# Twelve block products of a feed-forward layer ahead of its activation sums, with the memory pools around them laid out anew

## The chip, the cores and the metric

The kernel runs on one core of a Trainium2 chip. The metric is the device time of one execution in microseconds (us); the time before is the median of three runs. Engines are named as in the profile: PE is TensorE's matmul (PEld its weight load), DVE is VectorE, ACT is ScalarE, POOL is GpSimd, SP is SyncE, which here only issues transfers. L1197 is line 1197 of the kernel before.

## What is computed

One decoder layer over 1024 tokens of width 1024, all in float32. A token mixer (two groups of attention heads) ends in an output projection; its result is normalised, scaled and added to the input. A SwiGLU feed-forward with 2816 hidden features follows. Of the reference, the part that matters here:

```
y = concat(o_a, o_b) @ w_out
x = x + ga_m * rms_norm(y) * g_post_mix
h = rms_norm(x) * g_pre_ffn * (1 + sc_f) + sh_f
gate, up = split(h @ w_gate_up)
x = x + ga_f * rms_norm((silu(gate) * up) @ w_down) * g_post_ffn
```

## The kernel before

**Float32 as pairs.** Every matrix operand is split into a high part (a cast, L118 on ACT or L120 on DVE/POOL) and a low part (the difference, L121, on DVE or POOL). A product of two such operands takes three matmuls (hi·hi, hi·lo, lo·hi), each 128x128 weights on 512 columns.

**The planner.** The program is written as a sequence of tile operations. A planner with a cost model puts them into one fixed order per engine: among the operations that it takes to be ready, the one written first goes first. Each engine's queue then runs in that order, and the transfers that an engine issues stand in its queue too (SP most loads, ACT the `yd` loads and the stores). A tile waits until the earlier holders of its buffer, or of the same addresses, are done.

**Memory.** Pools lie on two stacks, `L` from the left and `R` from the right. During the last attention part (its `dsa_` pools fill most of `R`) the left stack already holds `fraw` (7 raw weight tiles), `fsum` (4 weight sums) and `fab0` (4 split weight blocks), then `outp`. `h2` (5 spaces of 16 KB per partition) lies on `R`, over the addresses of the attention's `dsa_hi`, which is used to the end of attention.

**The front stage** (L1069 to L1153) runs from the end of attention to the feed-forward:
- `WO`: the second half of w_out, 8 loads of 256 KB (L1092), split into the spaces `s1`, `s2` of `h2`.
- Eight token tiles (loop at L1103). For each: load the other half's result `yd` and `x`; split the attention output (`ohl`, into space `s4`); 24 matmuls into one bank of `ps_S` and one of `ps_O` (2 and 3 banks); two adds (L1120), two squares on ACT (L1121), small statistics and a power on POOL, multiplication with the gate `G_m` (L1125, mostly POOL), the update (L1129) and its store to `x2d`, a third square (L1131), and the scaling by 1/rms (L1133, DVE). `yt` has two buffers (space `s3`), `xt` five.
- After tile 3, eight transposed and modulated rows (`mod`, L1101, ACT) give the float32 copy `HB` and the split blocks `B11`, `B21` of the first 512 tokens.
- After tile 7, four steps k (L1142 to L1152) make the sums of a Strassen-Winograd scheme from both token halves: per step two `mod`, three sums on DVE, one on POOL, and five splits into `T1` to `T4` and `B22`.

**The feed-forward's first part** (L1156 to L1248, here called the main loop). For each of 22 feature tiles f, seven block products named "1" to "7" replace eight, each 12 matmuls (L1197). Their weights are two raw halves of gate, two of up, and four sums of them made on POOL (L1175 to L1178, `sources`); `prepare` splits a block 8 products ahead (ACT, DVE) into `fab0` (4 buffers) or `fab1` (6). Products "1" and "2" are gate times `B11` and `B21`: they need no sum, neither of weights nor of activations. "1" leaves a partial result `p1`, "2" completes it and gives silu of the first token half. The other five take `T2`, `T3`, `T1`, `T4`, `B22`. In `order` the "1" and "2" of f = 0 and 1 stand first. Each f stores 512 KB of `actd`.

**The second part** (the down projection, L1256 on) loads w_down (`wdr`, L1268) and `actd` (`adr`), splits them into `wd` and `ac`, and multiplies. Its pools `dw`, `da`, `dr`, `df` go on the left stack after `fraw` to `fca` are gone, `dr` over the lower end of `h2`, where `T3`/`T4` lie.

Of the kernel before, what the change touches and what calls it, by code (L numbers as in the profile page):

```python
# [13 lines left out]
P = 128  # L14
# [33 lines left out]
def hybrid_layer(ctx, tc, x, c, w_ada, b_ada, g_pre_mix, g_post_mix, g_pre_ffn, g_post_ffn, w_in,  # L48
# [1023 lines left out]
    fab = [L.push("fab0"), None]  # L1072
    op_ = L.push("outp")
# [5 lines left out]
    def space(tag):  # L1079

        return h2p.tile([P, 4096], F32, name="sp" + tag, tag=tag)

    WO = [space("s1").bitcast(F32R), space("s2").bitcast(F32R)]
    WO = [w.rearrange("p (k j d) -> p k j d", k=2, j=2) for w in WO]
    sp3, sp4 = space("s3"), space("s4")
    rawo = sp3[:, 0:2048].rearrange("p (b d) -> p b d", b=4)
# [8 lines left out]
    x2s = []  # L1095
    HB = op_.tile([P, KT, 512], F32, name="HB")
# [6 lines left out]
    for t in range(NT):  # L1103
# [3 lines left out]
        xt = op_.tile([P, D], F32, name="xt2", bufs=5)  # L1107
# [27 lines left out]
        if t == 3:  # L1135
            for k in range(KT):
                mod(HB[:, k, :], k, tr_k(x2s, k))
                b = (B11, B21)[k // KH_]
                split(b[:, k % KH_, 0, :], b[:, k % KH_, 1, :], HB[:, k, :], V, V if k % 2 else G)
    B22 = block(otp[1], "o")  # L1140
    T1, T2, T3, T4 = (block(h2p, "s%d" % j) for j in (1, 2, 3, 4))
    for k in range(KH_):  # L1142
        tm = [op_.tile([P, 512], F32, name=f"tm{j}") for j in range(6)]
        b12, b22, t1, t2_, t3, t4 = tm
        mod(b12, k, tr_k(x2s[4:], k))
        mod(b22, k + KH_, tr_k(x2s[4:], k + KH_))
        V.tensor_tensor(t1, b12, HB[:, k, :], op=OP.subtract)
        V.tensor_tensor(t2_, b22, t1, op=OP.subtract)
        G.tensor_tensor(t3, b22, b12, op=OP.subtract)
        V.tensor_tensor(t4, HB[:, k + KH_, :], t2_, op=OP.subtract)  # L1150
        for b, src, e in ((T2, t2_, V), (T3, t3, G), (T1, t1, V), (T4, t4, V), (B22, b22, G)):
            split(b[:, k, 0, :], b[:, k, 1, :], src, S, e)  # L1152
# [7 lines left out]
    FAB = (4, 6)  # L1160
# [3 lines left out]
    srcs, blks = {}, {}  # L1164

    def sources(f):

        r = {}
        for u in range(2):
            for h in range(2):  # L1170
                r[u, h] = fraw.tile([P, KH_, P], F32, name="rawg", bufs=7)
                nc.sync.dma_start(r[u, h], w_gate_up[0, h * 512:(h + 1) * 512, u * DFF + f * P:u * DFF + (f + 1) * P]
                                  .rearrange("(a p) n -> p a n", a=KH_))
        s1, s2, s3, s4 = (fsum.tile([P, KH_, P], F32, name=f"sw{j}") for j in range(4))
# [6 lines left out]
    def prepare(n):  # L1181
# [5 lines left out]
        b = int(n % sum(FAB) >= FAB[0])  # L1187
        blk = fab[b].tile([P, 2, KH_, P], F32R, name="wgu", bufs=FAB[b])
# [3 lines left out]
    def product(bank, n, w):  # L1192

        blk, hb = blks.pop(n), HBK[w]
        for k in range(KH_):
            for a, b in ((0, 0), (0, 1), (1, 0)):
                PE.matmul(bank, blk[:, a, k, :], hb[:, k, b, :], start=w in "165" and k + a + b == 0,  # L1197
                          stop=k == KH_ - 1 and a == 1, skip_group_check=True)

    def half_t(name, nb):  # L1200
        return fca.tile([P, 512], F32, name=name, bufs=nb)

    st_ = {}
# [3 lines left out]
    for n, (f, w) in enumerate(order):  # L1207
        prepare(n + LOOK)
        q = st_.setdefault(f, {})
        if w == "1":  # L1210
            q["X"] = ps_S()
            product(q["X"], n, w)
            q["p1"] = half_t("p1", 3)
            S.copy(q["p1"], q["X"])
        elif w == "2":
            product(q["X"], n, w)
            q["act"] = fca.tile([P, SEQ], F32, name="act", bufs=3)
            S.activation(q["act"][:, 0:512], q["X"], AF.Silu)
        elif w == "6":
            q["Z"] = ps_T()  # L1220
            product(q["Z"], n, w)
            q["u2"] = half_t("u2", 2)
            V.tensor_tensor(q["u2"], q["Z"], q["p1"], op=OP.add)
        elif w == "7":
            product(q["Z"], n, w)
            q["u3"] = half_t("u3", 2)
            V.tensor_tensor(q["u3"], q["Z"], q["p1"], op=OP.add)
        elif w == "5":
            q["W"] = ps_O()
            product(q["W"], n, w)  # L1230
# [12 lines left out]
        if w == "3" and f == 3:  # L1243
            acc5 = fca.tile([P, D], F32, name="act", bufs=3)
            with low(ADALOW):
                ada_acc(5, acc5, fraw, "rawg", 512, 7, nc.sync)
        if w == "3" and f == 6:
            ada_sum(5, acc5)  # L1248
    for name in ("fca", "fab1", "fab0", "fsum", "fraw"):
        L.pop(name)  # L1250
# [112 lines left out]
```

## Time and profile before

| | us |
|---|---|
| median of 3 runs (lowest, highest) | 1627.02 (1625.99, 1630.45) |
| profiled execution, its own time | 1627.21 |
| its span, first to last instruction | 1625.3 |
| PE busy | 1480.6 (91% of the span) |
| DVE, ACT, POOL busy | 1105.2, 847.9, 791.0 |

The profiled execution's time is 1.9 us more than its span, and 0.2 us from the median. Matmuls are pipelined: one that shows 389 ns starts 0.227 us after the one before it, so starts, not durations, tell the pace.

### The profile page before, as it was taken

How to read it: one execution, taken by the hardware profiler on the slowest of the kernel's cores; microseconds unless marked ns; L12 is line 12 of the kernel's file. 1: busy time of each engine (PE TensorE's matmuls, PEld its weight loads, DVE VectorE, ACT ScalarE, POOL GpSimd, SP SyncE). 2: the span in 40 equal slices, each digit the busy share in tenths (PEclk: the TensorE clock that was granted, in tenths of full speed). 3: DMA queues.
4: the chain of work that ended last, by engine and by line, in shares of the span. 5: the costliest groups of instructions: out<-in, count | busy, mean ns of one | idle time of the engine just before them, and what ended most of it. 6: DMA issues, size and time to landing. Idle time of an engine off the chain costs nothing. (4 is left out here: it accounts for less than half of the span.)

```text
span 1625.3 us, 23560 instructions
## 1 busy us (share of the span) xinstructions
PE 1480.6 (91%) x7973; PEld 1254.0 (77%) x7973; DVE 1105.2 (68%) x2476; ACT 847.9 (52%) x1802; POOL 791.0 (49%) x1046
## 2 busy tenths in 40 slices
PE   3899999987899998999978469999999998999998
PEld 3788999986677877788867358788888886888886
DVE  6888898989989997788746685845445453424422
ACT  3547588857778777778644443223323322432421
POOL 2584344548776655465536665544444442422320
PEclk9999999998999999999989679999999999999999
DMA  9461341200000002101253212622222214744721
GB/s 305 146 213 27 86 124 56 64 7 7 10 8 1 12 1 87 39 33 53 79 188 129 91 52 91 192 79 80 85 78 85 78 52 162 259 143 151 245 78 65
DMA packets 119913, 151.88 MB, mean 93 GB/s; under 512 B 15648, under 2 KB 83584, under 8 KB 119664
## 3 DMA queue, kind: packets, MB, share of 16 engines
q1 hardware_dynamic: 105856, 118.94, 23.6%
q10 hardware_dynamic: 13296, 29.30, 5.0%
q0 software_dynamic: 640, 2.13, 0.4%
q8 instruction: 63, 1.03, 0.3%
q14 instruction: 58, 0.48, 0.1%
HBM read 122.25 MB, written 28.09 MB: 93 GB/s over the span
## 5 line engine op out<-in xcount | busy, mean ns | idle before, releaser
L1197 PE MATMUL pT<-hbs,wgu 128*128 128x512 f32 x792 | 192.5, 393 | 16.9 <-ACT wgu L118 14.1
L1197 PEld LDWEIGHTS pT<-hbs,wgu 128*128 128x128 f32 x792 | 149.8, 190 | 49.8 <-ACT wgu L118 14.5
L742 DVE TENSOR_TENSOR ptl<-pT,ptl 128x512 fp32r<-128x512 f32 x228 | 139.5, 626 | 29.3 <-ACT ptl L741 28.1
L121 DVE TENSOR_TENSOR wd<-wdr,wd 128x512 fp32r<-128x512 f32 x88 | 68.3, 822 | 105.9 <-ACT wd L118 105.4
L741 ACT CAST ptl<-pT 128x512 fp32r<-128x512 f32 x228 | 117.5, 540 | 38.8 <-PE pO L842 17.6
L118 ACT CAST wgu<-sw 128x512 fp32r<-128x512 f32 x88 | 53.9, 621 | 145.8 <-PE pT L1197 81.6
L272 PE MATMUL pO<-wsp,hT 128*128 128x256 f32 (+1 forms) x416 | 121.2, 293 | 7.6 <-DVE hT L120 2.6
L273 PE MATMUL pO<-wsp,hT 128*128 128x256 f32 (+1 forms) x416 | 120.6, 291 | 5.1 <-DVE wsp L121 5.1
L274 PE MATMUL pO<-wsp,hT 128*128 128x256 f32 (+1 forms) x416 | 120.0, 289 | 0.0
L825 POOL TENSOR_SCALAR p<-p,stat,gates 128x640 f32<-128x640 f32 (+7 forms) x128 | 106.2, 843 | 23.2 <-DVE stat L737 17.7
L121 POOL TENSOR_TENSOR ac<-adr,ac 128x512 fp32r<-128x512 f32 x44 | 61.5, 1399 | 112.8 <-ACT ac L118 110.4
L732 ACT ACTIVATE p<-p,stat 128x640 f32<-128x640 f32 (+7 forms) x128 | 93.9, 736 | 26.7 <-DVE stat L731 17.2
L118 ACT CAST wd<-wdr 128x512 fp32r<-128x512 f32 x88 | 50.2, 619 | 102.6 <-PE pO L274 78.6
L121 DVE TENSOR_TENSOR wgu<-sw,wgu 128x512 fp32r<-128x512 f32 x88 | 78.7, 903 | 33.0 <-ACT wgu L118 27.2
L1235 POOL TENSOR_TENSOR act<-act,p 128x512 f32<-128x512 f32 x22 | 36.8, 1673 | 128.7 <-DVE p L1234 112.4
L538 ACT ACTIVATE tk_j<-scores,tk_s 128x384 bf16<-128x384 f32 (+2 forms) x93 | 87.1, 936 | 11.0 <-DVE tk_s L480 3.5
L272 PEld LDWEIGHTS pO<-wsp,hT 128*128 128x128 f32 x416 | 81.9, 198 | 9.3 <-ACT wsp L118 2.7
L273 PEld LDWEIGHTS pO<-wsp,hT 128*128 128x128 f32 x416 | 82.0, 198 | 6.7 <-DVE wsp L121 5.8
L121 DVE TENSOR_TENSOR wgu<-rawg,wgu 128x512 fp32r<-128x512 f32 x66 | 61.1, 929 | 36.9 <-ACT wgu L118 36.8
L470 DVE TENSOR_SCALAR_CACHE_REDUCE tk_j<-scores,tk_v 128x512 bf16<-128x512 f32 (+2 forms) x96 | 83.9, 874 | 1.1 <-DMA mkd<-tk_j 0.5
L721 PE MATMUL pS<-KK,qst 128*128 128x512 f32 (+3 forms) x192 | 76.1, 402 | 8.3 <-DVE stat L729 7.9
L837 PE MATMUL pT<-ident,p 128*128 128x128 f32 x528 | 81.7, 277 | 1.7 <-DVE ptl L742 1.2
(465 smaller groups left out, 4661.3 us busy)
## 6 DMA issues: line engine op xcount, KB each, us to landing
rawg<-in_w_gate_up_dram SPq DMA_DIRECT2D x88, 256.0 KB, 3.0
wdr<-in_w_down_dram SPq DMA_DIRECT2D x44, 512.0 KB, 5.1
actd<-act ACTq DMA_DIRECT2D x22, 512.0 KB, 2.6
adr<-actd SPq DMA_DIRECT2D x44, 256.0 KB, 3.6
raw<-in_w_in_dram SPq DMA_DIRECT2D x36, 256.0 KB, 2.9
xt<-in_x_dram SPq DMA_DIRECT2D x16, 512.0 KB, 5.7
wt<-in_w_ada_dram SPq DMA_DIRECT2D x32, 256.0 KB, 4.5
wt<-in_w_ada_dram SPq DMA_DIRECT2D x16, 512.0 KB, 5.0
```

The lines of the kernel that those rows point to most:

```text
L118: S.copy(hi, src)
L121: elo.tensor_tensor(lo, src, hi.bitcast(F32), op=OP.subtract)
L272: PE.matmul(o, lh, rh, start=first, stop=False)
L273: PE.matmul(o, lh, rl, start=False, stop=False)
L274: PE.matmul(o, ll, rh, start=False, stop=last)
L470: V.tensor_scalar(tkj[0][:, :w], score(i0 + j), thr(j), 0.0, op0=op, op1=OP.add, accum_out=cnt[:, j:j + 1])
L538: S.activation(tkj[1][:, :(i0 + j + 1) * P], score(i0 + j), AF.Sign, bias=ff[:, j:j + 1], accum_out=sg[:, j:j + 1])
L732: S.activation(p_, p_, AF.Exp, bias=stat[:, 0, r:r + 1], scale=-1.0, accum_out=stat[:, 1, r:r + 1])
L741: S.copy(hl[:n_rows, 0, :width], src[:n_rows, :width])
L742: V.tensor_tensor(hl[:n_rows, 1, :width], src[:n_rows, :width], hl[:n_rows, 0, :width].bitcast(F32), op=OP.subtract)
L825: G.tensor_scalar(self.p4[:, r, :n], self.p4[:, r, :n], stat[:, 2, r:r + 1], gates[:, i, c0 + r:c0 + r + 1], op0=OP.mult, op1=OP.mult)
L1197: PE.matmul(bank, blk[:, a, k, :], hb[:, k, b, :], start=w in "165" and k + a + b == 0, stop=k == KH_ - 1 and a == 1, skip_group_check=True)
```

## The change

- `early(f)`, for f = 0 to 5: products "1" and "2" of six feature tiles are written into the front stage, three among token tiles 5 to 7, three among the steps k = 0 to 2. Both results (`pr`, a tile of 512 KB) are stored to `early_d` in DRAM and loaded back as `p1` and `act` when the main loop comes to f. `order` is then five products for f < 6 and seven for the others: 142 in place of 154.
- `WO`, and after it `T1` and `B22`, get a pool of their own, `sl`, on the left stack under `outp`; `ohl` uses `fab0`'s buffers, which the early weights share; w_out's raw tiles use `fraw`; `yt` (and the sums' temporaries) three buffers `tm` in `outp`.
- The gate multiplication is one DVE operation per tile, the 1/rms scaling goes from DVE to ACT, `HB`'s splits go to ACT and DVE, the sums are written in place and all on DVE, and every split there is ACT and DVE; `WO`'s low parts are all on POOL.
- In the second part `dw` goes on the right stack, `dr` lowest on the left, then `da` and `df`.
- The ada columns (16 loads, DVE work) move from f = 3 and 6 to f = 8 and 11.

```diff
+    sl = L.push("sl")
     op_ = L.push("outp")
...
+    def wblock(b=0):
+        return fab[b].tile([P, 2, KH_, P], F32R, name="wgu", bufs=FAB[b])
+    def raw_w():
+        return fraw.tile([P, KH_, P], F32, name="rawg", bufs=7)
+    def pair():
+        return fsum.tile([P, 2, 512], F32, name="pair", bufs=2)
+    FAB = (4, 6)
+    EARLY = 6
+    early_d = dram.tile([EARLY, P, 2, 512], F32, name="earlyd")
-    WO = [space("s1").bitcast(F32R), space("s2").bitcast(F32R)]
+    WO = [sl.tile([P, 2, 2, D], F32R, name="WO" + tag, tag=tag) for tag in ("s1", "s2")]
...
-            raw = rawo[:, (2 * k + j) % 4, :]
+            raw = raw_w().rearrange("p a b -> p (a b)")
-            split(WO[k // 2][:, k % 2, 0, d], WO[k // 2][:, k % 2, 1, d], raw, S, V if k % 2 else G)
+            split(WO[k // 2][:, k % 2, 0, d], WO[k // 2][:, k % 2, 1, d], raw, S, G)
...
-        yt = sp3[:, 2048 + 1024 * (t % 2):3072 + 1024 * (t % 2)]
+        yt = op_.tile([P, D], F32, name="tm", bufs=3)
-        ohl = sp4[:, 1024 * (t % 2):1024 * (t % 2) + 1024].bitcast(F32R).rearrange("p (j k q) -> p j k q", j=2, k=4)
+        ohl = wblock()
-            e = V if j and t % 2 == 0 else G
-            e.tensor_tensor(yt[:, d], yt[:, d], G_m[:, d], op=OP.mult)
+        V.tensor_tensor(yt, yt, G_m, op=OP.mult)
-        V.tensor_scalar(xt, xt, r2, None, op0=OP.mult)
+        S.activation(xt, xt, AF.Copy, scale=r2)
...
+    def weights(n):
+        f, h = n // 2, n % 2
+        raw = raw_w()
+        nc.sync.dma_start(raw, w_gate_up[0, h * 512:(h + 1) * 512, f * P:(f + 1) * P]
+                          .rearrange("(a p) n -> p a n", a=KH_))
+        blk = wblock()
+        split(blk[:, 0], blk[:, 1], raw, S, V)
+        return blk
+    def early(f):
+        ws = [weights(2 * f + h) for h in range(2)]
+        bank = ps_O() if f % 2 else ps_S()
+        pr = pair()
+        product(bank, ws[0], B11, True, False)
+        S.copy(pr[:, 0], bank)
+        product(bank, ws[1], B21, False, True)
+        S.activation(pr[:, 1], bank, AF.Silu)
+        nc.scalar.dma_start(early_d[f], pr)
+    for t in range(4):
+        out_tile(t)
+    for k in range(KT):
+        mod(HB[:, k, :], k, tr_k(x2s, k))
+        b = (B11, B21)[k // KH_]
+        split(b[:, k % KH_, 0, :], b[:, k % KH_, 1, :], HB[:, k, :], S, V)
+    for t in range(4, NT):
+        out_tile(t)
+        if t > 4:
+            early(t - 5)
...
+        V.tensor_tensor(t1, b12, t1, op=OP.subtract)
+        V.tensor_tensor(b12, b22, b12, op=OP.subtract)
+        split(B22[:, k, 0, :], B22[:, k, 1, :], b22, S, V)
+        V.tensor_tensor(b22, b22, t1, op=OP.subtract)
+        V.tensor_tensor(t4, t4, b22, op=OP.subtract)
+        for b, src in ((T2, b22), (T3, b12), (T1, t1), (T4, t4)):
+            split(b[:, k, 0, :], b[:, k, 1, :], src, S, V)
+        if k < EARLY - 3:
+            early(k + 3)
...
-    order = [(0, "1"), (1, "1"), (0, "2"), (1, "2")] + [(f, n) for f in (0, 1) for n in "67543"]
-    order += [(f, n) for f in range(2, NF) for n in "1627543"]
+    order = [(f, n) for f in range(NF) for n in ("67543" if f < EARLY else "1627543")]
...
+            if f < EARLY:
+                q = st_[f] = {"p1": half_t("p1", 3), "act": act_t()}
+                nc.sync.dma_start(q["p1"], early_d[f, :, 0])
+                nc.sync.dma_start(q["act"][:, 0:512], early_d[f, :, 1])
...
-    dw = L.push("dw")
+    dw = R.push("dw")
+    dr = L.push("dr")
     da = L.push("da")
-    dr = L.push("dr")
     df = L.push("df")
```

## Rows read from the trace of the kernel before

**Rows 1.** Windows (start:end, length, busy by engine, PEclk, DMA share, GB/s): front, main loop, passage.
```profile
829.00:949.40 120.40, 71.59 (x282) 53.43 (x280) 78.50 (x83) 52.24 (x103) 67.92 (x72) 0.78 0.35 124
949.40:1370.90 421.50, 418.71 (x1840) 345.49 (x1840) 223.41 (x279) 125.20 (x215) 187.06 (x128) 0.99 0.30 93
1370.90:1382.20 11.30, 6.46 (x16) 4.97 (x16) 7.70 (x8) 7.07 (x13) 6.32 (x5) 0.70 0.77 276
```
**Rows 2.** Timeline of PE in the front stage (in brackets idle before, and releaser).
```profile
829.00 0.39 PE L274 MATMUL pO<-WOh,ohl 128*128 128x512 f32 x1
...
844.87 0.73 PE L272 MATMUL pS<-sps,sps 128*128 128x512 f32 x2 [2.96 <-ACT sps L118]
...
912.60 5.44 PE L1197 MATMUL pS<-hbo,wgu 128*128 128x512 f32 x12 [2.50 <-ACT pS L1121]
...
949.45 0.80 PE L1197 MATMUL pT<-hbs,wgu 128*128 128x512 f32 x1 [14.13 <-ACT wgu L118]
```
**Rows 3.** Timeline of SP, the queue that loads weights and x.
```profile
784.96 31.82 SPq L1172 DMA_DIRECT2D rawg<-in_w_gate_up_dram  x9
824.91 1.81 SPq L1092 DMA_DIRECT2D sps<-in_w_out_dram  x4
...
839.14 1.56 SPq L1092 DMA_DIRECT2D sps<-in_w_out_dram  x3
```
**Rows 4.** Windows inside the front stage: waiting for w_out, tiles, the four sum steps.
```profile
829.00:845.00 16.00, 9.40 (x27) 6.43 (x26) 3.91 (x4) 4.52 (x8) 3.07 (x3) 0.79 0.97 344
845.00:905.00 60.00, 49.31 (x215) 37.96 (x215) 40.80 (x47) 25.43 (x55) 39.70 (x47) 0.96 0.33 121
...
921.00:949.40 28.40, 6.21 (x23) 4.21 (x23) 26.89 (x24) 17.51 (x30) 18.52 (x12) 0.50 0.00 0
```
**Rows 5.** Timeline of DVE in the sum steps.
```profile
943.00 1.75 DVE L1147 TENSOR_TENSOR tm<-tm,HB 128x512 f32<-128x512 f32 x1
944.67 0.68 DVE L121 TENSOR_TENSOR hbs<-tm,hbs 128x512 fp32r<-128x512 f32 x1
```
**Rows 6.** Timeline of PE from the main loop's end into the down projection.
```profile
1356.18 2.88 PE L1197 MATMUL pS<-hbs,wgu 128*128 128x512 f32 x12
1358.90 2.88 PE L1197 MATMUL pO<-hbs,wgu 128*128 128x512 f32 x12
...
1365.36 3.01 PE L1197 MATMUL pT<-hbs,wgu 128*128 128x512 f32 x12 [0.85 <-DVE u L1227]
1368.21 2.88 PE L1197 MATMUL pO<-hbo,wgu 128*128 128x512 f32 x12
1375.93 0.80 PE L272 MATMUL pS<-wd,ac 128*128 128x512 f32 x1 [4.84 <-ACT ac L118]
```
**Rows 7.** Groups of ACT in the front stage: count, busy us, mean ns, idle before.
```profile
L118 ACT CAST hbs<-tm 128x512 fp32r<-128x512 f32 x16 | 9.5, 616 | 9.7 <-DVE tm L1147 6.7 <-DVE tm L1150 2.1 <-DVE tm L1148 0.8
L1131 ACT ACTIVATE sps<-xt 128x1024 f32<-128x1024 f32 x8 | 8.5, 1060 | 19.9 <-DVE xt L1129 9.8 <-DVE hbs L120 7.4 <-POOL rzv L125 2.6
...
L1101 ACT ACTIVATE HB<-pT,B_f,A_f 128x512 f32<-128x512 f32 x8 | 5.8, 775 | 2.7 <-PE pT L185 2.7
...
L1121 ACT ACTIVATE pS<-sps 128x512 f32<-128x512 f32 x8 | 4.8, 600 | 9.4 <-DVE sps L1120 9.4
...
L1121 ACT ACTIVATION_READ_ACCUMULATOR pS<-sps 128x1 f32 x8 | 1.5, 189 | 0.0
```
**Rows 8.** Groups of DVE in the front stage.
```profile
L1129 DVE SCALAR_TENSOR_TENSOR xt<-sps,ryr,xt 128x1024 f32<-128x1024 f32 x8 | 11.2, 1407 | 9.7 <-POOL ryr L1128 9.7
...
L1133 DVE TENSOR_SCALAR xt<-xt,rzr 128x1024 f32<-128x1024 f32 x8 | 6.0, 753 | 9.6 <-DMA x2d<-xt 6.7 <-POOL rzr L127 2.8
```
**Rows 9.** Groups of DVE, then of POOL, in the main loop, 1040 to 1340 us.
```profile
L121 DVE TENSOR_TENSOR wgu<-sw,wgu 128x512 fp32r<-128x512 f32 x64 | 57.3, 901 | 27.8 <-ACT wgu L118 23.3 <-POOL sw L1175 3.4
...
L1234 DVE TENSOR_TENSOR p<-pT,p 128x512 f32<-128x512 f32 x16 | 11.1, 692 | 43.7 <-PE pT L1197 43.7
...
L1235 POOL TENSOR_TENSOR act<-act,p 128x512 f32<-128x512 f32 x16 | 27.8, 1735 | 79.5 <-DVE p L1234 79.5
```

More of the change, by code (lines that the diff above doesn't have):

```diff
@@ L1101, in mod, with out_tile @@
         S.activation(dst, pt, AF.Identity, bias=B_f[:, k:k + 1], scale=A_f[:, k:k + 1])
-    for t in range(NT):
+    def out_tile(t):
         tk_ = slice(t * P, (t + 1) * P)
-        yt = sp3[:, 2048 + 1024 * (t % 2):3072 + 1024 * (t % 2)]
+        yt = op_.tile([P, D], F32, name="tm", bufs=3)
         nc.scalar.dma_start(yt, yd[tk_, :])
-        xt = op_.tile([P, D], F32, name="xt2", bufs=5)
+        xt = xt2s.pop() if xt2s else op_.tile([P, D], F32, name="xt2", bufs=5)
         nc.sync.dma_start(xt, x[0, tk_, :])
-        ohl = sp4[:, 1024 * (t % 2):1024 * (t % 2) + 1024].bitcast(F32R).rearrange("p (j k q) -> p j k q", j=2, k=4)
+        ohl = wblock()
         split(ohl[:, 0], ohl[:, 1], OT[1][:, :, tk_], S, V)
@@ L1132, in hybrid_layer @@
         r2 = rstd_of(op_, ss[:, 1:2], D, "rz")
-        V.tensor_scalar(xt, xt, r2, None, op0=OP.mult)
+        S.activation(xt, xt, AF.Copy, scale=r2)
         x2s.append(xt)
[L1135 to L1141, printed above, removed]
+    def weights(n):
[6 more added lines that the diff above has]
+        return blk
@@ new lines, in product @@
+    def product(bank, blk, hb, first, last):
+        for k in range(KH_):
+            for a, b in ((0, 0), (0, 1), (1, 0)):
+                PE.matmul(bank, blk[:, a, k, :], hb[:, k, b, :], start=first and k + a + b == 0,
+                          stop=k == KH_ - 1 and a == 1, skip_group_check=True)
+    def early(f):
[7 more added lines that the diff above has]
+        nc.scalar.dma_start(early_d[f], pr)
@@ L1142, in hybrid_layer @@
+    for t in range(4):
[8 more added lines that the diff above has]
+            early(t - 5)
+    T2 = block(otp[1], "o")
+    T3, T4 = (block(h2p, "s%d" % j) for j in (3, 4))
+    T1, B22 = (block(sl, "s%d" % j) for j in (1, 2))
     for k in range(KH_):
-        tm = [op_.tile([P, 512], F32, name=f"tm{j}") for j in range(6)]
@@ L1144, in hybrid_layer @@
-        b12, b22, t1, t2_, t3, t4 = tm
+        b12, b22 = (lambda m: (m[:, 0:512], m[:, 512:1024]))(op_.tile([P, D], F32, name="tm", bufs=3))
+        t1, t4 = HB[:, k, :], HB[:, k + KH_, :]
         mod(b12, k, tr_k(x2s[4:], k))
         mod(b22, k + KH_, tr_k(x2s[4:], k + KH_))
[L1147 to L1150, printed above, removed]
@@ L1159, in hybrid_layer, with half_t, act_t @@
     fca = L.push("fca")
-    FAB = (4, 6)
     HBK = {"1": B11, "2": B21, "3": B22, "4": T4, "5": T1, "6": T2, "7": T3}
-    order = [(0, "1"), (1, "1"), (0, "2"), (1, "2")] + [(f, n) for f in (0, 1) for n in "67543"]
-    order += [(f, n) for f in range(2, NF) for n in "1627543"]
+    order = [(f, n) for f in range(NF) for n in ("67543" if f < EARLY else "1627543")]
     srcs, blks = {}, {}
+    st_ = {}
+    def half_t(name, nb):
+        return fca.tile([P, 512], F32, name=name, bufs=nb)
+    def act_t():
+        return fca.tile([P, SEQ], F32, name="act", bufs=3)
     def sources(f):
@@ L1170, in sources @@
             for h in range(2):
-                r[u, h] = fraw.tile([P, KH_, P], F32, name="rawg", bufs=7)
+                r[u, h] = raw_w()
                 nc.sync.dma_start(r[u, h], w_gate_up[0, h * 512:(h + 1) * 512, u * DFF + f * P:u * DFF + (f + 1) * P]
                                   .rearrange("(a p) n -> p a n", a=KH_))
-        s1, s2, s3, s4 = (fsum.tile([P, KH_, P], F32, name=f"sw{j}") for j in range(4))
+        s12, s34 = pair(), pair()
+        s1, s2, s3, s4 = (s[:, j].rearrange("p (a b) -> p a b", a=KH_) for s in (s12, s34) for j in range(2))
         G.tensor_tensor(s1, r[1, 0], r[1, 1], op=OP.add)
@@ L1186, in prepare @@
             srcs[f] = sources(f)
-        b = int(n % sum(FAB) >= FAB[0])
-        blk = fab[b].tile([P, 2, KH_, P], F32R, name="wgu", bufs=FAB[b])
+            if f < EARLY:
+                q = st_[f] = {"p1": half_t("p1", 3), "act": act_t()}
+                nc.sync.dma_start(q["p1"], early_d[f, :, 0])
+                nc.sync.dma_start(q["act"][:, 0:512], early_d[f, :, 1])
+        blk = wblock(int(n % sum(FAB) >= FAB[0]))
         split(blk[:, 0], blk[:, 1], srcs[f][w], S, V)
         blks[n] = blk
[L1192 to L1203, printed above, removed]
     LOOK = 8
@@ L1242, in hybrid_layer @@
             st_.pop(f)
-        if w == "3" and f == 3:
-            acc5 = fca.tile([P, D], F32, name="act", bufs=3)
+        if w == "3" and f == 8:
+            acc5 = act_t()
             with low(ADALOW):
                 ada_acc(5, acc5, fraw, "rawg", 512, 7, nc.sync)
-        if w == "3" and f == 6:
+        if w == "3" and f == 11:
             ada_sum(5, acc5)
-    for name in ("fca", "fab1", "fab0", "fsum", "fraw"):
+    for name in ("fca", "fab1", "sl", "fab0", "fsum", "fraw"):
         L.pop(name)
@@ L1308, in hybrid_layer @@
                 nc.sync.dma_start(out[0, tk_, d], xt[:, d])
-    for name in ("df", "dr", "da", "dw"):
+    for name in ("df", "da", "dr"):
         L.pop(name)
+    R.pop("dw")
     L.pop("lpad")
```

39 lines of the change are left out of this document (14 added, 25 removed).

## The prediction

> **What bounds the kernel now.** I read the page's first part (the table above): PE is busy 91% of the span, so work taken off PE's busy stretches pays, and work put into its idle ones is free as long as the others keep pace. The windows say where the idle time is [rows 1]. In the front stage, 120.4 us, PE is busy 71.6 us at a granted clock of 0.78, that is 71.6 x 0.78 = 55.8 us of work at full clock: 65 us are lost. In the main loop it is busy 418.7 of 421.5 us at 0.99, with DVE at 53% and ACT at 30%: there time follows PE's work. The passage to the down projection has 6.5 busy of 11.3 us.
>
> PE's timeline then says what it waits for in the front [rows 2]: at 829.0 attention ends; it stops for w_out's splits up to 844.9; it has 14.13 us of idle ahead of the main loop's first product at 949.45. The finer windows give three parts [rows 4]: 16 us of waiting for w_out (27 matmuls, worth 27 x 0.227 = 6.1 us, so 9.9 lost); 60 us of tiles in which PE is busy 49.3; the four sum steps, 28.4 us, in which DVE is busy 26.9 and PE 6.2 at the low level of its clock (granted 0.50, 1.2 GHz). So the front is a chain over ACT, POOL and DVE with PE as a guest, and only the main loop is PE's.
>
> **The change, part by part.**
>
> *Twelve products leave the main loop's stretch; two of them stood in the front already.* A product of 12 matmuls takes 1358.90 - 1356.18 = 2.72 us in the loop [rows 6]. Of the 24 matmuls of L1197 ahead of 949.4 the last twelve are one row [rows 2]; the other twelve are the other "1". So the loop loses 10 products: **-27.2 us**, if the front takes them without growing.
>
> *What the front must carry.* PE: 55.8 us of work plus 120 matmuls x 0.227 = 27.2, sum 83. ACT [rows 7]: per tile a cast 0.616, two squares 0.600, three readouts 0.189, the third square 1.060, and the new scaling, which no row shows; by the nearest, the square of the same 128x1024, 1.060, so 4.5 us, x8 = 36; HB 8 x (0.775 + 0.616) = 11.1; the early blocks 12 x 0.616 = 7.4 and 12 evacuations at the squares' 0.600 = 7.2; the sums 8 x 0.775 + 20 x 0.616 = 18.5. Sum 80 against 52.2 now. DVE, uncontended [rows 5, 8]: per tile a split and two adds at 0.68, the 1024-wide gate product and update at 1.41 each, 4.9 us, x8 = 39; HB's splits 5.4, the early ones 8.2, the sums 4 x 9 x 0.68 = 24.5; sum 77 against 78.5. The three are nearly equal, so none alone sets the front's end below 829 + 83 = 912.
>
> *How long it then takes, by its parts.* w_out: its loads were issued from 824.9, three of them only at 839.1, because raw tiles and target lie over attention's last pool, while weight loads into `fraw` went out from 785.0 [rows 3]. Now they go where those went, and its splits can run during attention's last matmuls: the 9.9 us go. Tile part: 921 - 829 - 9.9 = 82 us if nothing else changes. The three early products in it need 3 x 5.44 = 16.3 us of PE at full clock; PE has 60 - 49.3 idle in the first stretch alone and more in the 16 us behind it, so they fit. Sum part: DVE 24.5, or ACT 18.5 + 3 x (2 x 0.616 + 2 x 0.600) = 25.8, so 26 in place of 28.4: POOL no longer takes part, and a sum on DVE took 1.75 us beside POOL and a split 0.68 without it [rows 5]. 829 + 82 + 26 = 937. Between 912 and 937 I take 931, nearer to the sum of parts, since tiles are chains; the 6 us are for the third `yt` buffer and the gate products that leave POOL. **B: -18.5 us** (bounds -37.5 and, with the front as long as now, 0).
>
> The Trainium skill (ScalarE: Activation LUTs, Rules for kernel authors) says to put copies and multiplications on VectorE, not ScalarE, which speaks against the scaling's move. The scaling took 0.753 on DVE [rows 8]; the square on ACT took 1.060 [rows 7]. By the rule, back on DVE, ACT would carry 80 - 8.5 = 72 and DVE 77 + 6 = 83; the sum stays where it is, since 83 is PE's load too.
>
> *The transfers moved and added.* The front carries 124 GB/s x 120.4 us = 14.9 MB; 12 weight loads of 256 KB come forward on SP, 6 stores of 512 KB come new on ACT's queue: 6.3 MB more, 21.2 MB in some 102 us, 208 GB/s, and 829 to 845 moved 344 [rows 1, 4]. They hide behind the splits and sums; without that cover, at 344 GB/s, 6.3 MB are 18 us. In the loop 3.1 MB come back, well ahead of use, beside a DMA share of 0.30. What stands behind them: on SP the `x` loads of tiles 5 to 7, which wait for HB's transposes (five buffers, as before); on ACT the next tile's `yd`. Cost taken: 0.
>
> *The main loop's first six tiles* need five products, 13.6 us. POOL has six operations per tile, at most 1.735 each [rows 9], 10.4. DVE has five splits at 0.90 and five adds at 0.69, 8.0. So PE keeps the lead. But "6" and "7" now follow each other in one bank, with DVE's read between them; such a wait was 0.85 us once at the loop's end [rows 6]. Six times would be 5.1; other ready blocks can be put between, as they were: **E: +1.5** (0 to 5.1).
>
> *The passage.* The loop's last matmul would end its slot at 1368.21 + 2.72 = 1370.93; PE went on at 1375.93 [rows 6], 5.0 us idle, and then 16 matmuls took 6.3 us instead of 16 x 0.227 = 3.6 [rows 1]: 7.7 lost. Now the raw tiles lie over `fraw`, free when the last block is split, 8 products before the end, and `wd` over blocks of which most are done by then. I take **D: -6** (0 if `wd`'s first buffer meets a block of the last product, to -7.7).
>
> The ada move (the same 16 loads and DVE work, five tiles later) I cost at nothing: DVE is at 53% in the loop [rows 1], and PE's products cover it.
>
> **Sum.** 1625.3 - 27.2 - 18.5 + 1.5 - 6 = 1575.1 us of span; the profiled run's own time is 1.9 above its span, and within 0.2 of the median: **1577**. Every such figure below is worked out in this way.
>
> **Rivals.**
> - *The front as long as before* (main loop from 949.45): the tile chain, not w_out or POOL, sets it, and ACT's load of 80 instead of 52 eats what the parts above give back. For it: ACT was already what PE waited for [rows 2]. Against: 9.9 us of the old front were w_out alone. Time 1577 + 18.5 = 1595.
> - *The first six tiles starve.* POOL's load rises from one tile in 19.1 us to one in 13.6. If each of five splits meets a POOL operation in full, 0.69 + 1.735, and five adds take 0.69, DVE needs 15.6 us per tile: 2.0 over, x6 = 12, time 1589. For it: the splits already show 0.90 instead of 0.68 [rows 5, 9]. Against: the adds, which read PSUM, show no stretching. The Trainium skill (SBUF — State Buffer, SBUF: two separate sides) has DVE and GpSimd lock one port pair for a whole instruction when DVE reads two SBUF operands; the rows agree (0.90 against 0.69), and by the rule 15.6 is the worst case too.
> - *The planner doesn't move them.* The early blocks' operations are ready late, their order ends up behind the sums, and the front plus loop keeps its work: only D and part of w_out come. 1627.2 - 6 - 5 = 1616.
> - *Slower: the early products stand in series with the chain.* `ohl` and early weights share four buffers, the evacuations wait in ACT's queue, and each pair blocks a token tile or a sum step: per pair 2 x (2.72 + 2.50, PE's wait for ACT ahead of a "1" [rows 2]) = 10.4, x6 = 63, less w_out's 9.9: the loop starts at 1002, and the time is 1577 + 71 = 1648. Decided at a start of 949.45 + 27.2 + 6 - 1.5 = 981: slower if over 42 of the 63 us are not hidden. For it: at the low clock a product took 5.44 us [rows 2]. Against: PE has over 60 idle us there.
>
> **How the numbers follow.** Forecast 0.58 (its own range 1557 to 1588), front as before 0.20, starving 0.07, not moved 0.07, in series 0.08. The range 1557 to 1606 reaches from the forecast's dense end (start at 912, 1558) over the front as before with the passage unchanged as well (1601) and E at its worst; "not moved" and "in series" are left out. A difference under 0.3% (5 us) can't be told from none here. Faster: the first three, and the larger part of the fourth, 0.89; same 0.04; slower 0.07.
>
> **What would show it.** PE's first matmul on `WO` within 2 us of attention's end (w_out); first product "6" around 931 (B); DVE's sums at 0.68; products at 2.72 us spacing in f < 6, no idle over 1 us (E); under 2 us of idle ahead of the first `wd` matmul (D). Wrong would be: a loop start after 950, PE waits on `wgu` in f < 6, or early products at 5.4 us that hold up `ohl`.

## The result, and the profile after

The changed kernel takes 1585.74 us (median of 4 runs, 1583.1 to 1592.74), the kernel before, beside it, 1626.51 (1624.04 to 1630.45): a ratio of 0.975, interval 0.973 to 0.977. The forecast was 1577; the time is 8.7 us above it, inside the likeliest case's own range. The profiled execution is the slowest of the four: 1592.74 us, span 1591.0, and it reaches the first `oev` add of the last attention part (L1047) at 675.1 us, 3.7 later than the kernel before did.

Windows of the changed kernel: front up to the first product of the main loop, that loop's first 17 us, the loop, and the passage (start:end, length, busy of PE, PEld, DVE, ACT, POOL, then PEclk, DMA share, GB/s). They answer to [rows 1].
```profile
829.00:943.03 114.03, 93.96 (x420) 75.95 (x418) 69.08 (x93) 69.64 (x132) 42.03 (x48) 0.91 0.53 182
943.03:960.00 16.97, 12.97 (x36) 9.25 (x37) 15.53 (x17) 8.24 (x15) 10.20 (x6) 0.70 0.55 172
943.03:1340.49 397.46, 393.46 (x1720) 324.52 (x1721) 217.83 (x279) 121.64 (x209) 188.16 (x130) 0.99 0.34 106
1340.49:1350.00 9.51, 6.76 (x23) 5.18 (x22) 8.24 (x8) 1.77 (x3) 5.85 (x5) 0.82 0.82 300
```
The front ends 6.4 us earlier (943.03 for 949.45), the loop is 421.5 - 397.5 = 24.0 us shorter, and what follows its last product is 3.9 shorter (1591.0 - 1340.5 = 250.5 for 254.4): together the 34.3 us between the spans. The second profile of the changed kernel (span 1585.4, nearer the median; below) has 9.2, 25.3 and 5.4. In the front PE is now busy 94 of 114 us and no longer a guest. The loop's 142 products would take 142 x 2.72 = 386.2 us; 11 more are lost, some 9 of them before 960: 36 matmuls run in those 17 us, at a granted clock of 0.70, where the kernel before ran 61 in its loop's first 17 us.

Windows inside the front and the loop, which answer to [rows 4]:
```profile
829.00:845.00 16.00, 16.00 (x73) 12.94 (x72) 8.01 (x10) 4.01 (x9) 5.15 (x5) 1.00 0.58 177
845.00:905.00 60.00, 50.53 (x214) 40.54 (x213) 36.15 (x45) 40.35 (x77) 24.07 (x35) 0.89 0.60 215
905.00:932.00 27.00, 27.00 (x133) 22.29 (x132) 17.02 (x26) 20.36 (x38) 2.91 (x5) 1.00 0.49 160
932.00:960.00 28.00, 13.40 (x40) 9.44 (x39) 23.42 (x31) 13.15 (x24) 20.11 (x8) 0.71 0.39 129
960.00:1320.00 360.00, 360.00 (x1596) 298.32 (x1595) 196.33 (x254) 107.38 (x183) 173.69 (x120) 1.00 0.35 108
```
The wait for w_out is gone: 73 matmuls in the first 16 us instead of 27. (Part of them is attention's. Its last matmul on `VD` starts at 838.51 here, before at 826.79: 36 matmuls on `WO` now run ahead of it, and this profile is 3.7 us late.) From 905 to 932 PE does nothing but work at full clock, and DVE is busy only 17 of those 27 us. From 960 on, the loop is PE's without a gap.

PE's timeline at the points that the prediction named, in answer to [rows 2, 6]:
```profile
851.43 0.73 PE L272 MATMUL pS<-WOs,wgu 128*128 128x512 f32 x1 [4.91 <-ACT pS L1129]
...
924.53 1.47 PE L185 MATMUL pT<-ident,xt 128*128 128x128 f32 x12
925.76 3.01 PE L1157 MATMUL pS<-hbs,wgu 128*128 128x512 f32 x12
928.60 0.60 PE L185 MATMUL pT<-ident,xt 128*128 128x128 f32 x4
928.96 3.03 PE L1157 MATMUL pO<-hbs,wgu 128*128 128x512 f32 x12
931.82 0.60 PE L185 MATMUL pT<-ident,xt 128*128 128x128 f32 x4
943.03 1.22 PE L1157 MATMUL pT<-hbo,wgu 128*128 128x512 f32 x2 [10.60 <-ACT wgu L118]
...
960.31 3.14 PE L1157 MATMUL pT<-hbs,wgu 128*128 128x512 f32 x12
963.29 2.88 PE L1157 MATMUL pO<-hbs,wgu 128*128 128x512 f32 x12
...
1346.59 0.80 PE L272 MATMUL pO<-wd,ac 128*128 128x512 f32 x1 [2.75 <-DVE u L1275]
```
Two things are new. At 851 PE waits 4.9 us behind tile 0's adds. And the last transposes (L185), which the sum steps start from, stand among early products up to 932; the main loop then waits 10.6 us for its first weights.

What is behind those two waits, on the timelines of ACT's queue, DVE and POOL:
```profile
843.85 1.54 ACTq L1114 DMA_DIRECT2D tm<-yd  x3
...
849.93 0.69 DVE L1128 TENSOR_TENSOR tm<-tm,pS 128x512 f32<-128x512 f32 x1 [4.74 <-DMA tm<-yd]
...
928.94 0.68 DVE L1189 TENSOR_TENSOR HB<-tm,HB 128x512 f32<-128x512 f32 x1
929.54 0.69 DVE L121 TENSOR_TENSOR hbo<-tm,hbo 128x512 fp32r<-128x512 f32 x1
...
933.05 7.94 POOL L1226 TENSOR_TENSOR pair<-rawg 128x512 f32<-128x512 f32 x1 [17.96 <-ACT tm L1109]
941.06 1.26 POOL L1227 TENSOR_TENSOR pair<-pair,rawg 128x512 f32<-128x512 f32 x1
...
942.35 0.62 ACT L118 CAST wgu<-pair 128x512 fp32r<-128x512 f32 x1 [6.12 <-POOL pair L1227]
```
The first `yd` loads are issued only at 843.85, since their `tm` buffers lie in `outp`, over memory that attention holds to its end; so the wait for w_out gave way to a shorter one for `yd`. At the other end the main loop's first weight sum takes 7.94 us on POOL, where the next takes 1.26, beside a DVE that does one sum or split after another, 0.60 us apart.

### The profile page after: what moved, and what is told of

Read it like the earlier page. It is cut to its first block, busy times and chain, and to the rows that moved or that the text cites. A ratio compares the mean times of both kernels' runs of the same rounds, so it can differ in the third digit from the quotient of the medians.

```text
span 1591.0 us, 23592 instructions
## 1 busy us (share of the span) xinstructions
PE 1476.6 (93%) x7973; PEld 1256.1 (79%) x7973; DVE 1083.2 (68%) x2476; ACT 858.3 (54%) x1818; POOL 765.0 (48%) x1022
## 3 DMA queue, kind: packets, MB, share of 16 engines
q1 hardware_dynamic: 113920, 125.24, 25.3%
## 4 chain that ended last, share of the span: by engine, by line
PE 63%; DVE 19%; DMA 6%; ACT 6%; issue 3%; POOL 3%; ACTq 0%; SPq 0%; DVEq 0%; POOLq 0%
PE pT L1157 11%; PE pO L1157 8%; PE pS L1157 6%; PE pO L272 4%; PE pO L274 4%; PE pO L273 4%; DVE p L729 3%; DVE tk_j L470 3%; DVE ptl L742 2%; PE pT L837 2%; DMA wt<-in_w_ada_dram 2%; PE pS L721 2%; PE pT L274 2%; PE pT L272 2%; PE pT L273 2%
## 5 line engine op out<-in xcount | busy, mean ns | idle before, releaser
L1157 PE MATMUL pO<-hbs,wgu 128*128 128x512 f32 x564 | 137.7, 391 | 1.4 <-ACT wgu L118 1.4
L118 ACT CAST wgu<-pair 128x512 fp32r<-128x512 f32 x88 | 53.5, 621 | 151.7 <-PE pT L1157 69.0
L1157 PE MATMUL pT<-hbs,wgu 128*128 128x512 f32 x528 | 127.1, 390 | 0.0
L1157 PEld LDWEIGHTS pO<-hbs,wgu 128*128 128x128 f32 x564 | 106.3, 189 | 24.2 <-ACT wgu L118 2.1
L1157 PEld LDWEIGHTS pT<-hbs,wgu 128*128 128x128 f32 x528 | 99.4, 188 | 20.8
L121 DVE TENSOR_TENSOR wgu<-pair,wgu 128x512 fp32r<-128x512 f32 x88 | 76.0, 874 | 31.6 <-ACT wgu L118 29.1
L272 PEld LDWEIGHTS pO<-wsp,hT 128*128 128x128 f32 x416 | 81.9, 198 | 10.6 <-ACT kvt L607 3.7
```

What stands on the lines that cost most here:

```text
L118: S.copy(hi, src)
L121: elo.tensor_tensor(lo, src, hi.bitcast(F32), op=OP.subtract)
L272: PE.matmul(o, lh, rh, start=first, stop=False)
L1157: PE.matmul(bank, blk[:, a, k, :], hb[:, k, b, :], start=first and k + a + b == 0, stop=k == KH_ - 1 and a == 1, skip_group_check=True)
```

## The experiments

All twelve runs were timed in five rounds beside the kernel before, whose median was 1626.3 to 1627.8 us in the three batches. Intervals of the ratios are about +-0.002, some 3.5 us: a smaller difference between two versions is not told apart by their times. Between versions of different batches, the difference of the medians and that of the ratios (times 1627) lie up to 3 us apart; both are given where it matters. Stages are counted from attention's last matmul on `VD`, the same point in all versions; "front products" are those written ahead of the main loop (the order of before puts two there); in three of the versions with products behind the transposes PE runs the last one after that loop's first.

| version | front products | median us | ratio, 95% interval | last WO matmul | last transpose | first `wd` matmul |
|---|---|---|---|---|---|---|
| changed kernel again | 12 | 1587.07 | 0.9749 [0.9726, 0.9771] | 68.6 | 94.0 | 501.0 |
| f=0's weight sums on DVE | 12 | 1588.62 | 0.9755 [0.9734, 0.9776] | 68.7 | 94.0 | 500.0 |
| no early products | 2 | 1596.93 | 0.9803 [0.9781, 0.9825] | 47.0 | 72.9 | 507.9 |
| down pools of before | 12 | 1595.17 | 0.9800 [0.9777, 0.9823] | 66.1 | 91.5 | 504.5 |
| f=3 to 5 behind the transposes | 12 | 1583.16 | 0.9734 [0.9721, 0.9748] | 68.8 | 84.9 | 500.3 |
| same, own buffers | 12 | 1580.90 | 0.9728 [0.9707, 0.9749] | 66.2 | 83.2 | 495.1 |
| only f=0 to 2 early | 6 | 1599.75 | 0.9838 [0.9823, 0.9853] | 68.5 | 86.8 | 513.9 |
| first `yd` loads into pairs | 12 | 1577.03 | 0.9704 [0.9686, 0.9723] | 59.8 | 85.1 | 491.1 |
| both: `yd`, behind | 12 | 1574.82 | 0.9677 [0.9654, 0.9701] | 60.0 | 76.9 | 488.4 |
| `yd`, no early products | 2 | 1594.66 | 0.9803 [0.9780, 0.9826] | 40.3 | 70.3 | 506.4 |
| `yd`, six in the sum part alone | 6 | 1583.12 | 0.9720 [0.9697, 0.9743] | 39.0 | 69.2 | 492.7 |
| no early, sums shared with POOL | 2 | 1604.78 | 0.9861 [0.9836, 0.9885] | 48.2 | 74.0 | 515.9 |

**The changed kernel once more**, as the base of the others.

> The changed kernel itself, unchanged, beside the variants on one chip: 1583 to 1588 us (median so far 1585.7), ratio to the kernel before 0.973 to 0.977. Its profile should again show the main loop's first product near 943 us, some 10 us of idle PE ahead of it, and a POOL sum L1226 of about 8 us; if the long POOL sum is an accident of one execution, it will not come back.

Its profile (span 1585.4) has the same waits: 4.90 us at tile 0's adds, 10.61 ahead of the loop's first product at 940.24. So the picture above is no accident of one execution.

**The weight sums of f=0 on DVE.** The 7.94 us on POOL were the first suspect.
```
-        G.tensor_tensor(s1, r[1, 0], r[1, 1], op=OP.add)
...
+        e = V if f == 0 else G
+        e.tensor_tensor(s1, r[1, 0], r[1, 1], op=OP.add)
```


> The four weight sums of feature tile 0 (L1226 to L1229) run on DVE in place of POOL; nothing else changes. Theory port: the first sum took 7.94 us on POOL because DVE's unbroken stream of two-operand operations kept it out until 939.9; on DVE it takes 0.69, the first main-loop product comes at 935 to 938 in place of 943, and the time falls by 5 to 8 us, to 1578 to 1581. Rival late data: the sums wait for raw weights or for the buffer that the early pair's store frees (933 us) and the rest is only how the record looks; then the sums stand at 940 or later on DVE too, and the time stays at 1584 to 1588. If the ramp behind the start (idle and low clock up to 957) is not due to the sums, at most 5 us come back even under theory port.

No change (1588.62). The four sums took 0.68 us each, but they stood in DVE's stream, which had no gap above 0.1 us from 923 to 948, and the ramp remained. So POOL's long operation is not what costs the time; that DVE's stream as a whole sets the start fits this, and isn't shown by this run alone.

**No early products**, all else as changed.
```
-    EARLY = 6
+    EARLY = 0
...
+    order = [(0, "1"), (1, "1"), (0, "2"), (1, "2")] + [(f, n) for f in (0, 1) for n in "67543"]
```


> No early products: the new pools, engines and order of the front and of the down projection, but all 154 products in the main loop in the old order. Theory (the early products' price is 27.2 us of loop less what the front grows by): the front is shorter than with the early products, main loop start at 925 to 937, loop 27 us longer, time 1600 to 1612; the layout alone is then worth 15 to 26 us of the 41. Rival (the layout is worth little, the early products nearly all): main loop start at 943 or later, time 1612 to 1622. Other rival (the early products cost what they bring): 1583 to 1592, as with them.

1596.93: the new layout alone brings 1627.6 - 1596.9 = 30.7 us, the early products 9.9 more, for ten products that would cost 27.2 in the loop. PE's timeline shows what they could have filled:
```profile
893.34 0.44 PE L185 MATMUL pT<-ident,xt 128*128 128x128 f32 x2
901.98 0.90 PE L185 MATMUL pT<-ident,xt 128*128 128x128 f32 x3 [8.21 <-ACT xt L1140]
...
909.50 1.88 PE L185 MATMUL pT<-ident,xt 128*128 128x128 f32 x8 [0.22 <-ACT tm L1109]
928.41 4.36 PE L1157 MATMUL pT<-hbo,wgu 128*128 128x512 f32 x12 [17.02 <-ACT wgu L118]
```
Without them the loop starts at 928.4, earlier than the forecast's 931. PE's idle time lies behind the last tile's matmuls: 8.2 us for that tile's chain and 17.0 for the sum steps. Of the twelve products the changed kernel runs four ahead of those matmuls.

**The down projection's pools as before.**
```
-    dw = R.push("dw")
+    dw = L.push("dw")
+    da = L.push("da")
     dr = L.push("dr")
-    da = L.push("da")
     df = L.push("df")
```


> Only the pools of the down projection are put back as before (dw, da, dr, df all on the left stack in the old order); front and early products stay. Prediction's term D: the passage loses 5.0 us idle and up to 2.7 us at the low clock again, so the time rises by 4 to 8 us, to 1590 to 1594. Rival: the profile of the changed kernel lost 2.75 us of idle and a low clock a little later (at 1346), so D is worth 3 to 4 us net: 1588.5 to 1590. Rival: the passage is set by the last product's sums and not by the pools: no change, 1584 to 1588.

8.1 us slower than the changed kernel. PE's waits between 1325 and 1360 (total, times, longest), first in this version, then in the changed kernel's second profile:
```profile
PE pS L272 <- ACT ac L118: 8.7, 2, 6.9
```
```profile
PE pO L272 <- DVE u L1275: 2.7, 1, 2.7
```

**The six products of f=3 to 5 behind the last transpose.**
```
-        if k < EARLY - 3:
-            early(k + 3)
+    with tc.issue_after(tr_last[0].ins):
+        for f in range(3, EARLY):
+            early(f)
```


> The six products of tiles f=3 to 5 are issued after the last step of the sums, and on PE's queue behind the last transpose of the sum part; nothing else changes. Theory Q (PE's queue): in the changed kernel 28 of the sum part's last 32 transposes stand behind early products on PE and run from 910 to 932 us, where the version without early products has them done at 911; the sum steps wait for them. Then here the last transpose is over by about 917, the sums end some 8 to 10 us earlier, the main loop's first product starts near 933 to 936 us instead of 940 to 943, and the time is 1577 to 1581 us against 1587. Theory S (splits and evacuations): it is the early blocks' work on ScalarE and VectorE (12 casts of about 0.62 us and 12 subtractions of about 0.7 to 0.9 us) beside the sum steps that lengthens the part, whatever PE's order. Then the start stays at 940 or later and the time at 1585 to 1590.

Half of theory Q held. The last transposes come 9.1 us earlier (84.9 for 94.0), but the loop does not start earlier (106.0 us from attention's last matmul for 104.8); 1583.16 lies between the two forecasts, and its 3.9 us are about what times tell apart.

**The same, with buffers of their own** (`xt2` instead of the pairs that f=0's weight sums need).
```
+    PX = 3
...
-        pr = pair()
+        pr = pair() if f < PX else op_.tile([P, D], F32, name="xt2", bufs=5).rearrange("p (a b) -> p a b", a=2)
```


> As the version with the six products behind the last transpose, and the results of f=3 to 5 wait for their stores in the five buffers of the token tiles (xt2) instead of in the two pairs that the weight sums of the main loop's first tile need. Theory P (the pairs hold the start): the weight sums of f=0 start only when the last early pair is stored (933 us in the changed kernel); with buffers of their own they start as soon as their raw weights are there, the start comes 3 to 5 us before that of the version that shares the pairs, and the ramp after it is shorter: 1574 to 1578 us. Rival: the sums of f=0 fall into time that VectorE's sum steps set anyway, and their memory, which the second pool of blocks lies over, comes free later: within 2 us of the version that shares the pairs.

1580.90, 2.3 us below the version before and above theory P's range, so the times leave it open. Its timeline shows what sets the start once the transposes and the pairs don't. DVE has no gap from 916 to 943; PE, with eleven of its twelve early products done by 933, gets its blocks at DVE's pace. POOL's sums of f=0 now run early (913 to 919, 1.26 to 1.72 us each), and it is f=1's that are caught:
```profile
940.00 4.60 POOL L1228 TENSOR_TENSOR pair<-rawg 128x512 f32<-128x512 f32 x1 [20.55 <-DVE wgu L121]
944.68 1.26 POOL L1229 TENSOR_TENSOR pair<-pair,rawg 128x512 f32<-128x512 f32 x1
```
```profile
946.64 4.63 PE L1158 MATMUL pT<-hbo,wgu 128*128 128x512 f32 x12 [3.46 <-ACT wgu L118]
```

**Only f=0 to 2 early** (`EARLY = 3`).

> Only the six products of f=0 to 2 come early (those of the tile part); the other six run in the main loop as in the kernel before. Theory Q: only the two products of f=2 (5.4 us) stand before the last transposes, the start is near 932 to 935, the loop has six products of 2.72 us less than without early ones (1596.9 us, start 928.4): 1596.9 - 16.3 + 4 to 6 = 1585 to 1587, the same as with all twelve, because the last six cost in the start what they save in the loop. If the last six were worth their 16.3 us: 1596 or more. If they cost more than they save: under 1583.

A miss: 1599.75, no better than without any. I had counted six products saved, but two stand in the front anyway, so four are new, 10.9 us; and the tile part, 47.0 us without early products, takes 68.5 with six, as with twelve. Moreover the loop's first products all need sums here, and PE feeds on single blocks as they come:
```profile
922.86 1.22 PE L1157 MATMUL pO<-hbs,wgu 128*128 128x512 f32 x2 [1.23 <-DVE wgu L121]
...
933.70 1.65 PE L1157 MATMUL pT<-hbo,wgu 128*128 128x512 f32 x3 [1.56 <-DVE hbo L121]
...
943.18 1.22 PE L1157 MATMUL pT<-hbo,wgu 128*128 128x512 f32 x2 [2.24 <-ACT wgu L118]
```
From here to all twelve the time falls by 12.7 us for six products (16.3): those in the sum part pay, those in the tile part, with `yd` late, don't. The same six behind the transposes with buffers of their own (1580.90, same batch) bring 18.9.

**The first two `yd` loads into the pairs**, which are free during attention.
```
-        yt = op_.tile([P, D], F32, name="tm", bufs=3)
+        yt = pair().rearrange("p a b -> p (a b)") if t < 2 else op_.tile([P, D], F32, name="tm", bufs=3)
```


> The first two loads of the stored half projections (yd) go to the weight sums' pair buffers, which are free, instead of to tm buffers, which lie over memory of the attention. In the changed kernel VectorE waits 4.7 us for them and PE idles 4.9 us at 851 behind that. Theory Y: they land before 847, that idle goes, tiles and sums start some 4 us earlier and with them the main loop: 1582 to 1584 us. Rival: later tiles wait for tm buffers or for x, or the loads come no earlier, for they stand behind a wait on ScalarE's queue: 1586 to 1588 and the same start near 940.

1577.03, 10 us below the changed kernel by the medians, 7 by the ratios: more than theory Y gave. Windows 845 to 885, first the changed kernel's second profile, then this one:
```profile
845.00:885.00 40.00, 32.32 (x129) 25.97 (x130) 25.96 (x31) 26.42 (x54) 19.51 (x28) 0.81 0.58 200
```
```profile
845.00:885.00 40.00, 35.75 (x162) 29.63 (x161) 27.86 (x34) 31.17 (x63) 20.82 (x31) 0.91 0.57 210
```
The loads are issued at 807 to 809, and the PE idle of 4.9 us is gone. PE does 162 matmuls and transposes instead of 129 in the 40 us, though attention ends 3.5 us later in this profile: it is busy 3.4 us longer, and the granted clock is 0.91 instead of 0.81. In the changed kernel the clock falls to the lower level (1.2 GHz; granted 0.50 from 848.3 to 852.3) after the idle time, and nine matmuls then start 0.43 us apart instead of 0.23, as here in its second profile:
```profile
848.34 0.79 PE L272 MATMUL pS<-WOs,wgu 128*128 128x512 f32 x1 [4.90 <-ACT pS L1129]
848.93 0.63 PE L273 MATMUL pS<-WOs,wgu 128*128 128x512 f32 x1
849.36 0.63 PE L274 MATMUL pS<-WOs,wgu 128*128 128x512 f32 x1
```
The last WO matmul comes 8.8 us earlier.

**Both edits.**

> Two edits of before together: the first two yd loads into the pairs (1577.0 us alone, -10.0 against the changed kernel's 1587.1) and the six products of f=3 to 5 behind the last transpose with buffers of their own (1580.9 alone, -6.2). Theory A (two places: the first shortens the tile part, 65.7 to 56.9 us from attention's last projection to the last matmul of the tiles, the second the sum part): they add, 1570 to 1573 us. Theory B (both take time out of one chain, VectorE's, which is unbroken from the sums to the main loop's start): 1575 to 1577, no better than the yd loads alone.

1574.82, the fastest version: 12 us below the changed kernel. It lies just below theory B's range, but theory A isn't ruled out. Over the `yd` loads alone the second edit brings 2.2 us by the medians and 4.4 by the ratios, where alone it brought 6.2 and 3.4: by the ratios the two add. The last transpose comes 8 us earlier. The loop's start at 930.67 has no 10 us gap any more, and waits of only 0.4 us in its ramp:
```profile
930.67 2.20 PE L1158 MATMUL pT<-hbo,wgu 128*128 128x512 f32 x9
932.71 3.34 PE L1158 MATMUL pO<-hbs,wgu 128*128 128x512 f32 x14
...
939.37 0.73 PE L1158 MATMUL pT<-hbo,wgu 128*128 128x512 f32 x2 [0.38 <-ACT wgu L118]
```

**The `yd` loads first, no early products.**

> No early products, and the yd loads first. Theory T: with the yd loads late, the six early products of the tile part fall on a chain that is already behind, and lengthen the part by 21.7 us (44.0 without them, 65.7 with them; their own time at 2.72 us each is 16.3). The loads alone then give what PE idles for them without early products, 4 to 6 us of 1596.9: 1591 to 1593 us, and the twelve early products are worth 14 to 16 us beside early yd loads, against 10 without. Rival: the yd loads are worth 10 us whatever stands behind them: 1587, and the early products are worth 10 in both.

1594.66. Theory T in kind: alone the loads bring 2.3 us (0 by the ratios), not resolved; beside early products they bring 10.0 (7.3). The tile part shrinks by 6.7 us here too (40.3 for 47.0), but the last transpose only by 2.6. The early products are worth 1594.7 - 1577.0 = 17.6 us (16.1 by the ratios) once `yd` is on time, of 27.2.

**The `yd` loads first, six products in the sum part and none in the tile part.**

> Early products only for f=0 to 2, all six behind the last transpose, results in the token buffers, none in the tile part; the yd loads first. Theory T2: without products the tile part is about 40 us (44.0 less the wait for yd), the six run in the 17 us that PE idles before the main loop there and cost VectorE six subtractions of 0.6 to 0.7 us ahead of the start: no early ones with yd first (1591 to 1593) - 16.3 + 2 to 4 = 1577 to 1581 us, some 5 to 8 more than with twelve, because the tile part's six then bring a few us. Rival: the tile part's six cost as much as they save also with the yd loads first: within 2 us of the version with both edits and twelve products.

1583.12, 11.5 us below the version with none: all of the 10.9 that its four new products take in the loop. (The expectation subtracted 16.3, the same miscount.) The other six, in the tile part, bring the 8.3 us that still lie between this version and the fastest one, half of their 16.3.

**No early products, sum steps shared with POOL as before the change.**
```
-        V.tensor_tensor(b12, b22, b12, op=OP.subtract)
-        split(B22[:, k, 0, :], B22[:, k, 1, :], b22, S, V)
+        G.tensor_tensor(b12, b22, b12, op=OP.subtract)
+        split(B22[:, k, 0, :], B22[:, k, 1, :], b22, S, G)
...
-        for b, src in ((T2, b22), (T3, b12), (T1, t1), (T4, t4)):
-            split(b[:, k, 0, :], b[:, k, 1, :], src, S, V)
+        for b, src, e in ((T2, b22, V), (T3, b12, G), (T1, t1, V), (T4, t4, V)):
+            split(b[:, k, 0, :], b[:, k, 1, :], src, S, e)
```


> The version without early products (1596.9 us, main loop from 928.4), with three operations of each of the four sum steps back on GpSimd, as before the change (the subtraction b22-b12 and the low halves of two of the six splits). Theory V: VectorE's sums at 0.68 us each in an unbroken stream are what brought the start to 928; with GpSimd between them, its operations take 1.3 us or more and VectorE's beside them 1.75: the start is 3 to 8 us later, 1600 to 1605 us. Rival: the relief of VectorE (12 operations of 0.6 us, 7.2 us) outweighs it: start 924 to 928, 1592 to 1597.

1604.78, 7.9 us slower; the start relative to attention's end moves from 90.2 to 97.3. Theory V, by these rows of DVE and POOL:
```profile
907.76 1.72 POOL L121 TENSOR_TENSOR hbs<-tm,hbs 128x512 fp32r<-128x512 f32 x1
```
```profile
908.28 1.75 DVE L121 TENSOR_TENSOR hbs<-HB,hbs 128x512 fp32r<-128x512 f32 x1
909.95 1.75 DVE L1190 TENSOR_TENSOR tm<-tm,HB 128x512 f32<-128x512 f32 x1
...
913.30 0.68 DVE L1191 TENSOR_TENSOR HB<-HB,tm 128x512 f32<-128x512 f32 x1
```
A DVE operation beside one of POOL takes 1.75 us, one without 0.68. Moving twelve operations to POOL took 12 x 0.6 = 7 us from DVE and gave back more.

## Why the prediction was right or wrong

**Direction and size right, the makeup not.** The forecast put -27.2 on the loop, -18.5 on the front's end, -6 on the passage. By the runs the layout, passage included, brings 30.7 us, the early products 9.9. Against the forecast's stretches the miss is B's: in the second profile the front's end comes 9.2 us earlier instead of 18.5, the loop is 25.3 shorter (25.7 forecast, with E), and the rest 5.4 (6).

**The step that failed** stands in "How long it then takes, by its parts": the three pairs in the tile part need "3 x 5.44 = 16.3 us of PE at full clock", PE has that much idle, "so they fit", and the sum part takes 26 us in any case. The amount of idle time was right, its place wrong. Without early products the layout starts the loop at 928.4, near the predicted 931: B's size was right for that kernel. PE's idle 25 us lie after the last tile's matmuls, where the tile's chain and the sum steps run. The planner put two pairs of products and, ahead of them, the first half's transposes and splits that they need, before the last tile's matmuls, and eight more products among the transposes that the sums start from. In a fixed order that delays the chain behind which the idle time lay: tile part 47.0 to 68.6 us, last transpose 72.9 to 94.0, first product 928 to 940 or 943. That is the mechanism of the rival "in series" at a part of its price. (Of the "over 60 idle us" held against that rival, 120.4 - 71.6 = 48.8 are idle [rows 1]; the rest is the low clock.) That the products' place decides is shown: in the sum part and behind the transposes four new ones return 11.5 of 10.9 us, and six added to those of the tile part 18.9 of 16.3; in the tile part six return 8.3 of 16.3 at best. Within the sum part place mattered less: behind the transposes the six brought 3.9 us more with the pairs shared and 6.2 with buffers of their own (2.4 and 3.4 by the ratios), hardly resolved.

**The w_out wait**: right, it is gone (PE busy 16.00 of 16.00 us; the first matmul on `WO` runs at 827.68, before attention's last). Its 9.9 us went only in part, because the prediction did not ask when the new `tm` buffers come free: `yd` came 4.7 us late. Once early products queue on PE, that wait and the low clock behind it are worth 7 to 10 us; without them at most 2.3. I cost the `yd` transfers at 0.

**The sums on DVE at 0.68 us**: right (0.68 and 0.69 throughout), worth 7.9 us by the run that undoes it.

**E, +1.5**: the size nearly came out (27.2 - 24.0 = 3.2 and, in the second profile, 1.9), by luck, for the cause is another. The wait for the bank that E priced isn't there: from 960 to 1320 PE is busy 360.00 of 360.00 us, products 2.72 apart. What E left out is the ramp before 960: 36 matmuls in the loop's first 17 us (46 in the second profile) for 61 in the kernel before, some 3 to 6 us. Sum steps, first blocks and f=0's weight sums all end in DVE's stream or just behind it, at 940 to 950.

**D, -6**: -8.1 by the run with the old pools, -3.9 and -5.4 by the time behind the loop in the two profiles; the mechanism was right, and the size as far as these tell. PE goes on at 1340.49 without a gap. What is left is a wait of 2.75 us for a bank whose last sum DVE still reads, which I had not named.

**The scaling on ScalarE** was weighed and left at nothing. The Trainium skill (ScalarE: Activation LUTs, Rules for kernel authors) would put it on VectorE: the rule lists additions, multiplications, maxima and the like, not the copies that the prediction names beside them. No run here moved that operation alone, so this stays open. ACT's scaling took 1.15 us where DVE's took 0.753 [rows 8], so the prediction's 1.060 was a little low, and PE waits for it 8.2 us in the version without early products, as the end of a longer chain.

**Not separated** are the other parts of the layout's gain: 30.7 less 8.1 (passage) and 7.9 (sums) leaves some 15 us, an estimate that takes them to add, for w_out's loads, the third buffer and the gate products on DVE together.

## What to carry to other kernels

Idle time of an engine is worth only what fits behind the last instruction that others wait for: before moving work into it, find that instruction in the engine's fixed order, and see that the moved work, and all that the work itself needs, is put after it. A wait that cost little while the engine had slack costs its full length, and the slow clock behind it, once the slack is filled; so look again at what is late next after each fill. And test a change with several parts by undoing one at a time: here three quarters of the gain came from the layout (where buffers lie, and which engine does what), not from the products that were moved.

## What the runs showed of the hardware

A POOL operation that takes 1.26 us alone took 7.94 us (changed kernel) and 4.60 us (own buffers) where DVE ran operations on two SBUF operands without a gap, 0.60 us apart. Both ended 1.1 us after that stream did (939.87 and 940.99 in the first case, 943.48 and 944.60 in the second), as if each had begun its work only then. Late operands are not the reason in the first case: in the run with the sums on DVE the same sum ran at 933.15 in 0.68 us. The Trainium skill (SBUF — State Buffer, SBUF: two separate sides) says that of two such operations the one that starts first keeps the shared ports for its whole instruction. DVE's 1.75 us beside POOL's 1.72 agree with that. The 7.94 us go further: POOL was passed over not for one DVE instruction but for eleven, and the 4.60 for six, so in these two cases DVE's dense stream kept POOL out until it ended. How the port is granted can't be seen in a trace; it is inferred from these ends.
